# Differential attention's last rounds: p's parts, the key copies, the order of the end, and two weight splits

## The chip, the cores and the metric

The kernel runs on one core of one Trainium2 chip. The metric is the device time of one execution in microseconds. The kernel before has a median of 1311.96 us over three runs (1311.76 to 1312.21). Engines are named as in the profile: PE is TensorE, DVE is VectorE, ACT is ScalarE, POOL is GpSimd, SP is SyncE, which issues nearly all transfers here.

## The reference, cut to what matters

The program is a decoder trunk of two layers over 512 tokens of 1024 features. Layer 0 mixes tokens with a convolution, layer 1 with differential attention; each layer ends with a SwiGLU feed-forward part and a gated input embedding made from `p`. The change touches layer 1's attention, the projection of `p[1]`, and the first products with `w_o`:

```python
qkv = x @ w_qkv                                   # x is rms-normed
q = rms_norm(q per head half, q_g) * HEAD_DIM ** -0.5
k = rms_norm(k per head half, k_g)                # 8 heads, 2 halves (c) of 64
logits = einsum('bhcqd,bhckd->bhcqk', q, k) + bias, causal
w = softmax(logits)[c=0] - lam * softmax(logits)[c=1]
o = rms_norm(w @ v, sub_g) * (1 - lambda_init)    # per head, 128 wide
h = h + o @ w_o
...
h = h + sigmoid(rms_norm(h) @ ple_w_gate) * (p[1] @ ple_w_proj)
```

## The kernel before, in words

**Precision by parts.** Every operand of a large product is held as two fp32r parts, hi and lo, with hi + lo equal to the fp32 value. `mm3` (L153) makes a product of three matmuls: lo by hi, hi by lo, hi by hi. The parts of a weight come from `weight` (L138): SP loads a 128x1024 tile into `wraw` (two buffers), ACT copies it to `whi` (L149), and DVE, or POOL where `eng=G` is given, subtracts to make `wlo` (L150). `whi` and `wlo` have four buffers each, so at most four weights are ready at one time, and a buffer of `wraw` is free only when its subtraction is done.

**Order.** Instructions are written in program order; a planner with its own simulated times then decides in which order each engine gets them. Program order is the priority: an instruction written later may overtake where an earlier one isn't expected to be ready, and when a tile's buffer isn't free the instructions that need it wait. Once planned, each engine works through its queue in order. SP's queue holds the loads in the same way: a load that waits for a buffer of `wraw` holds back those behind it.

**Queries, keys, values.** Six slabs of four weights each (the table `QKV`, L81) run in the order q0, v0, q1, q2, v1, q3. A slab does four token blocks of 128 (`tb`); each block is 24 matmuls of 128x512 (`tokens`, L675). A value block is stored in its own tile `B0` to `B7` (`values`, L691): `B0` and `B1` are the first two blocks of heads 0 to 3. A q slab holds a pair of heads: after the block, ACT, DVE and POOL work out the norms (`unit`, L702), and one block later `unit_end` (L724) transposes on PE and writes the parts. For each half `c`, ACT writes the query's hi part (L735) and the key's hi part (L736) to 64 partitions, and then POOL copies the key's hi part to the other 64 partitions (L740, `KDUP = "G"`); DVE writes the two lo parts (L743, L745). The parts of a pair lie in tiles `C0` to `C5`, with two buffers each, so pairs 0 and 2 share one buffer, and pairs 1 and 3 the other.

**Attention.** The work of head `hd` and query block `qb` has three stages: `stage_s` (L752: scores on PE, L772 and L773; bias and minimum on DVE, L775; exponential on ACT, L779; three DVE steps L782 to L784), `stage_t` (L787: PE transposes L792, ACT and DVE make the parts L794 and L795) and `stage_a` (L801: products with the values L808 and L809; after the last block of a head the norm of the head, with POOL steps at L214 and L830). Round n holds the scores of item n, the transposes of item n-2, and the products of item n-3; there are 32 items, so rounds 0 to 34. `stage_o` (L834) transposes a finished head (L837) and splits it into `A` tiles. 63 of the 96 stages are placed between the matmuls of the six slabs (`pace`); 33 are left, from the last stage of round 22 on.

**The end of attention.** After the slabs, `pfeatures` (L249) loads the two halves of `p[1]` through `wraw` and writes their parts to tiles `C0` and `C1` (L253 on ACT, L254 on DVE). Then `project` (L259) makes the eight blocks of `p @ ple_w_proj`, six matmuls each, with two weights. Then `linear` (L537) does `o @ w_o`, the first two weights side by side over the eight heads. A call of `step()` (L873) takes one stage, and `stage_o` where a head is due; it stands before each block of `project`, twice inside it, and after each `mm3` of the first two `w_o` weights. These hooks are the arguments `before` and `after` of `linear`.

Of the kernel before, what the change touches and what calls it, by code (L numbers as in the profile page):

```python
# [13 lines left out]
F32R = mybir.dt.float32r  # L14
AF = mybir.ActivationFunctionType
# [5 lines left out]
P = 128  # L21
S = 512
D = 1024
NC = D // P
NH = 8
# [44 lines left out]
        TAPS += [(_c, j) for j in range(0, PE_TAPS[_c], 4)]  # L70


KDUP = "G"
HALVES = slice(0, DH), slice(DH, P)
LT = 2
LA = 3
# [8 lines left out]
def trunk(ctx, tc, xT, pT, wts, diag, dww, vec, rel, onehot, lamv, out):  # L85
    nc = tc.nc
    V, A, G, T = nc.vector, nc.scalar, nc.gpsimd, nc.tensor
# [7 lines left out]
    def sb(shape, tag, bufs, dt=F32):  # L95
        uid[0] += 1
        return pool.tile(shape, dt, tag=tag, name=f"{tag}_{uid[0]}", bufs=bufs)

    def ps(tag, bufs, shape=(P, S)):
        uid[0] += 1  # L100
        return psum.tile(list(shape), F32, tag=tag, name=f"{tag}_{uid[0]}", bufs=bufs)

    mm = lambda: ps("mm", 4)
# [4 lines left out]
    f = lambda ap: ap.bitcast(F32)  # L108
# [6 lines left out]
    def col(name, i=0):  # L115
        a, _ = VEC[name]
        return vt[:, a + i : a + i + 1]
# [7 lines left out]
    t = wk()[:, 0:P]  # L125
# [4 lines left out]
    t = tp()  # L130
# [7 lines left out]
    def weight(n=1024, pieces=1, between=(), eng=V):  # L138
        i = wnext[0]
        wnext[0] += 1  # L140
        raw = sb([P, 1024], "wraw", 2)
        hi = sb([P, 1024], "whi", 4, F32R)
        lo = sb([P, 1024], "wlo", 4, F32R)
        for k in range(pieces):
            cut = slice(k * n // pieces, (k + 1) * n // pieces)
            loaded[0] = nc.sync.dma_start(raw[:, cut], wts[i, :, cut])
            if k < len(between):
                between[k]()
            A.copy(hi[:, cut], raw[:, cut])  # L149
            eng.tensor_tensor(lo[:, cut], raw[:, cut], f(hi[:, cut]), ALU.subtract)  # L150
        return hi, lo

    def mm3(acc, a, b, first, last):  # L153
        (ah, al), (bh, bl) = a, b
        T.matmul(acc, al, bh, start=first, stop=False)  # L155
        T.matmul(acc, ah, bl, start=False, stop=False)  # L156
        return T.matmul(acc, ah, bh, start=False, stop=last)  # L157

    def wpart(w, k):
        return tuple(t[:, k * P : (k + 1) * P] for t in w)  # L160

    def both(t):
        return t[:, 0], t[:, 1]
# [4 lines left out]
    def split_scaled(src, scale, hi, lo):  # L168
        A.activation(hi, src, AF.Copy, scale=scale)  # L169
        V.scalar_tensor_tensor(lo, src, scale, f(hi), ALU.mult, ALU.subtract)  # L170
# [78 lines left out]
    def pfeatures(layer, parts):  # L249
        for k, (hi, lo) in enumerate(parts):  # L250
            raw = sb([P, 1024], "wraw", 2)[:, :S]
            nc.sync.dma_start(raw, pT[layer, :, k * S : (k + 1) * S])
            A.copy(hi, raw)  # L253
            (G if layer == 0 else V).tensor_tensor(lo, raw, f(hi), ALU.subtract)  # L254
        return parts

    ph = pfeatures(0, [(sb([P, S], t, 2, F32R), sb([P, S], t, 2, F32R)) for t in ("wth", "wtl")])

    def project(ph, m, w, o, step=lambda: None):  # L259

        acc = mm()
        for k in range(2):
            mm3(
                acc,
                wpart(w, 2 * (m % 4) + k),
                ph[k],
                k == 0,
                k == 1,
            )
            step()  # L270
        A.copy(o, acc)
        return o
# [239 lines left out]
    pp = []  # L512
    for m in range(NC):
        if m % 4 == 0:
            w = weight()
        with tc.issue_after((last_tap if m < 4 else last_moment)[0].ins):
            if m < 6:
                o = sb([P, S], f"D{m}", 1)
            elif m == 6:
                o2 = sb([P, 2, S], "C4", 2)  # L520
                o = o2[:, 0]
            else:
                o = o2[:, 1]
# [10 lines left out]
            if c >= 2:  # L534
                V.tensor_tensor(z[c - 2][1], y[c - 2], f(z[c - 2][0]), ALU.subtract)

    def linear(n_in, src, consume, group0=1, before=None, after=None, first=0):  # L537


        m = 0  # L540
        while m < NC:
            g = group0 if m == 0 else 1
            ws = [weight(n_in * P, eng=G if m == 0 and i >= g - first else V) for i in range(g)]
            accs = [mm() for _ in range(g)]
            for k in range(n_in):
                if before:
                    before(k)
                for w_, a_ in zip(ws, accs):
                    mm3(a_, wpart(w_, k), src[k], k == 0, k == n_in - 1)
                    if after:  # L550
                        after()
            for i in range(g):
                consume(m + i, accs[i])
            m += g
# [3 lines left out]
    def add_conv(m, acc):  # L558
        V.scalar_tensor_tensor(h[m], acc, col("b_pw2", m), h[m], ALU.add, ALU.add)
        norm.chunk(m)  # L560

    linear(NC, z, add_conv, 3, first=ZW)


# [73 lines left out]
    for k in range(2):  # L638
        t = tp()
# [27 lines left out]
    def slab(n=0):  # L667
        ws = [weight(eng=G if i < n else V) for i in range(4)]
        return [
            tuple(t[:, j * S : (j + 1) * S] for t in ws[k])  # L670
            for k in range(4)
            for j in range(2)
        ]
# [50 lines left out]
    def unit_end(pair, tb, q):  # L724
        t = tp()
        for i in range(4):
            T.transpose(t[:, i * P : (i + 1) * P], q[:, i * P : (i + 1) * P], ident)
        t4 = t.rearrange("p (h c t) -> p h c t", h=2, c=2)
        cut = slice(tb * P, (tb + 1) * P)
        qs, ks, kl = qk[pair][0:2], qk[pair][2:4], qk[pair][4:6]  # L730

        qg, kg = gains[:, 0:1], col("k_g")
        for c in range(2):
            own, other = HALVES[c], HALVES[1 - c]
            A.activation(qs[c][own, :, cut], t4[own, :, 0], AF.Copy, scale=qg[own])  # L735
            A.activation(ks[c][own, :, cut], t4[own, :, 1], AF.Copy, scale=kg[own])  # L736
            if KDUP == "A":
                A.activation(ks[c][other, :, cut], t4[own, :, 1], AF.Copy, scale=kg[own])
            else:
                G.tensor_copy(ks[c][other, :, cut], f(ks[c][own, :, cut]))  # L740
        for c in range(2):
            own, other = HALVES[c], HALVES[1 - c]
            V.scalar_tensor_tensor(  # L743
                qs[c][other, :, cut], t4[own, :, 0], qg[own], f(qs[c][own, :, cut]), ALU.mult, ALU.subtract)
            V.scalar_tensor_tensor(  # L745
                kl[c][own, :, cut], t4[own, :, 1], kg[own], f(ks[c][own, :, cut]), ALU.mult, ALU.subtract)
# [85 lines left out]
    ot = {}  # L832

    def stage_o(hd):  # L834
        t = tp()
        for i in range(4):
            T.transpose(t[:, i * P : (i + 1) * P], osb[hd][:, i * P : (i + 1) * P], ident)  # L837
        hi = sb([P, S], f"A{2 * hd}", 1, F32R)
        lo = sb([P, S], f"A{2 * hd + 1}", 1, F32R)
        split_scaled(t, gains[:, 1:2], hi, lo)  # L840
        ot[hd] = (hi, lo)
# [3 lines left out]
    stages = []  # L845
    for n in range(len(todo) + LA):
        for stage, at in ((stage_s, n), (stage_t, n - LT), (stage_a, n - LA)):
            if 0 <= at < len(todo):
                stages.append((n, partial(stage, *todo[at])))

    def take(n):
        got, stages[:n] = [s for _, s in stages[:n]], []
        return got

    waiting = None
    for what, at, pace in QKV:
        ws = slab(GLO if at > 0 else 0)
        for tb in range(4):
            between = take(3 * pace[tb])
            between += [None] * (6 - len(between))  # L860
            if waiting:
                between.append(partial(unit_end, *waiting))
                waiting = None
            if what == "v":
                values(at, ws, tb, between)
            else:
                waiting = unit(at, ws, tb, between)
    unit_end(*waiting)


    done = [0]

    def step():  # L873
        if stages:
            n, s = stages.pop(0)
            s()
        else:
            n = 99
        while done[0] < NH and (n - LA - 3) // 4 > done[0]:
            stage_o(done[0])  # L880
            done[0] += 1

    ph = pfeatures(1, [both(sb([P, 2, S], t, 2, F32R)) for t in ("C0", "C1")])
    pp = []
    for m in range(NC):
        if m % 4 == 0:
            w = weight()
        step()
        if m < 2:
            o = sb([P, S], f"D{m + 2}", 1)  # L890
        elif m % 2 == 0:
            o2 = sb([P, 2, S], f"C{m // 2 + 1}", 2)
            o = o2[:, 0]
        else:
            o = o2[:, 1]
        pp.append(project(ph, m, w, o, step))

    def heads_until(k):
        while done[0] <= k:
            step()  # L900

    norm = Norm("ffn_g1")

    def add_attn(m, acc):
        V.tensor_tensor(h[m], acc, h[m], ALU.add)
        norm.chunk(m)

    linear(NC, ot, add_attn, 2, heads_until, step)
    n2 = Norm("ple_g1")
    ffn(norm, n2)  # L910

# [131 lines left out]
```

## Time and profile before

| what | value |
|---|---|
| median of 3 runs | 1311.96 us (1311.76 to 1312.21) |
| the profiled execution's own time | 1313.88 us |
| its span in the trace, first to last instruction | 1312.1 us |
| PE busy, PEld busy | 1276.4 us (97%), 1047.4 us (80%) |
| DVE, ACT, POOL busy | 759.3, 526.9, 276.1 us |
| mean granted TensorE clock | 0.988 |
| data moved | 129.21 MB, 98 GB/s mean |

The profiled execution lies 1.92 us above the median, and 1.78 us above its own span. A row of the stage table gives the stretch of the span, its length, and the busy time of each engine with the number of its instructions in brackets; PEclk is the clock granted to TensorE as a share of full speed. In a row of the timeline stand the start, the duration, the engine, the line, the operation and the tiles; what stands in square brackets is the idle time of the engine just before, and who ended it. PE's busy time is modelled and overlaps, so that the distance from one matmul to the next, and not its duration, is what it costs.

### The profile page before, as it was taken

How to read it: one execution, taken by the hardware profiler on the slowest of the kernel's cores; microseconds unless marked ns; L12 is line 12 of the kernel's file. 1: busy time of each engine (PE TensorE's matmuls, PEld its weight loads, DVE VectorE, ACT ScalarE, POOL GpSimd, SP SyncE). 2: the span in 40 equal slices, each digit the busy share in tenths (PEclk: the TensorE clock that was granted, in tenths of full speed). 3: DMA queues.
4: the chain of work that ended last, by engine and by line, in shares of the span. 5: the costliest groups of instructions: out<-in, count | busy, mean ns of one | idle time of the engine just before them, and what ended most of it. 6: DMA issues, size and time to landing. Idle time of an engine off the chain costs nothing. (4 is left out here: it accounts for less than half of the span.)

```text
span 1312.1 us, 15285 instructions
## 1 busy us (share of the span) xinstructions
PE 1276.4 (97%) x5830; PEld 1047.4 (80%) x5830; DVE 759.3 (58%) x1168; ACT 526.9 (40%) x832; POOL 276.1 (21%) x219
## 2 busy tenths in 40 slices
PE   8999889999999999999999998999999999999998
PEld 5787668888888888888888886778888888888887
DVE  6998866544344434455678888945543344334445
ACT  5644255332123212253566767734332233223332
POOL 4839533000000000022345534122000000000030
PEclk8999889999999999999999998999999999999999
DMA  5554203332333232232222221213233323222231
GB/s 193 182 179 156 81 32 113 96 97 80 113 96 96 81 112 96 77 116 94 72 97 81 86 75 49 97 33 128 97 96 97 96 97 97 96 96 88 80 122 64
DMA packets 44534, 129.21 MB, mean 98 GB/s; under 512 B 5123, under 2 KB 8835, under 8 KB 44460
## 3 DMA queue, kind: packets, MB, share of 16 engines
q1 hardware_dynamic: 42912, 125.84, 29.2%
q10 hardware_dynamic: 1548, 2.39, 0.6%
q8 instruction: 46, 0.75, 0.2%
q14 instruction: 28, 0.23, 0.1%
HBM read 124.52 MB, written 3.69 MB: 98 GB/s over the span
## 5 line engine op out<-in xcount | busy, mean ns | idle before, releaser
L149 ACT CAST whi<-wraw 128x1024 fp32r<-128x1024 f32 (+2 forms) x214 | 218.5, 1026 | 563.5 <-PE mm L157 363.1
L155 PE MATMUL mm<-A,wlo 128*128 128x512 f32 (+1 forms) x1096 | 425.6, 392 | 9.5 <-ACT A L533 5.9
L156 PE MATMUL mm<-A,whi 128*128 128x512 f32 (+1 forms) x1096 | 428.9, 392 | 0.7 <-DVE A L170 0.5
L157 PE MATMUL mm<-A,whi 128*128 128x512 f32 (+1 forms) x1096 | 426.5, 390 | 0.0
L150 DVE TENSOR_TENSOR wlo<-wraw,whi 128x1024 fp32r<-128x1024 f32 (+2 forms) x207 | 257.5, 1248 | 66.6 <-ACT whi L149 66.2
L155 PEld LDWEIGHTS mm<-A,wlo 128*128 128x128 f32 x1096 | 207.2, 189 | 55.2 <-ACT A L533 6.7
L156 PEld LDWEIGHTS mm<-A,whi 128*128 128x128 f32 x1096 | 207.0, 189 | 48.0 <-DVE A L170 3.8
L157 PEld LDWEIGHTS mm<-A,whi 128*128 128x128 f32 x1096 | 207.0, 189 | 43.3 <-issue 1.3
L189 POOL TENSOR_TENSOR acc<-acc,wk 128x512 f32<-128x512 f32 x42 | 68.6, 1634 | 786.7 <-issue 673.3
L156 PE MATMUL mm<-B,whi 128*128 128x512 f32 x352 | 137.5, 391 | 0.0
L157 PE MATMUL mm<-B,whi 128*128 128x512 f32 x352 | 137.5, 391 | 0.0
L155 PE MATMUL mm<-B,wlo 128*128 128x512 f32 x352 | 137.1, 391 | 0.0
L591 DVE TENSOR_TENSOR h<-mm,h 128x512 f32<-128x512 f32 x48 | 33.0, 691 | 123.1 <-PE mm L157 123.0
L583 DVE TENSOR_TENSOR big<-mm,rb 128x512 f32<-128x512 f32 x44 | 30.4, 691 | 126.2 <-PE mm L157 126.2
L581 DVE TENSOR_TENSOR big<-mm,rb 128x512 f32<-128x512 f32 x44 | 30.4, 691 | 99.0 <-PE mm L157 92.6
L157 PEld LDWEIGHTS mm<-B,whi 128*128 128x128 f32 x352 | 66.1, 188 | 14.5
L156 PEld LDWEIGHTS mm<-B,whi 128*128 128x128 f32 x352 | 66.0, 188 | 14.3
L155 PEld LDWEIGHTS mm<-B,wlo 128*128 128x128 f32 x352 | 66.1, 188 | 14.2
L157 PE MATMUL mm<-whi,A 128*128 128x512 f32 x192 | 75.6, 395 | 0.0
L156 PE MATMUL mm<-wlo,A 128*128 128x512 f32 x192 | 75.0, 396 | 0.0
L155 PE MATMUL mm<-whi,A 128*128 128x512 f32 x192 | 74.8, 396 | 0.0
L214 POOL TENSOR_TENSOR r<-v,mhalf 128x8 f32<-128x8 f32 (+1 forms) x31 | 47.4, 1530 | 114.6 <-DVE v L212 92.4
(207 smaller groups left out, 1439.0 us busy)
## 6 DMA issues: line engine op xcount, KB each, us to landing
wraw<-in_wts SPq DMA_DIRECT2D x194, 512.0 KB, 3.5
wraw<-in_wts SPq DMA_DIRECT2D x16, 384.0 KB, 2.9
D<-in_diag SPq DMA_DIRECT2D x19, 256.0 KB, 4.7
C<-in_diag SPq DMA_DIRECT2D x12, 256.0 KB, 5.5
h<-in_xT SPq DMA_DIRECT2D x8, 256.0 KB, 5.3
bias<-scr ACTq DMA_DIRECT2D x8, 256.0 KB, 3.5
out_t<-h SPq DMA_DIRECT2D x7, 256.0 KB, 2.0
wraw<-in_wts SPq DMA_DIRECT2D x4, 256.0 KB, 4.8
```

The lines of the kernel that those rows point to most:

```text
L149: A.copy(hi[:, cut], raw[:, cut])
L150: eng.tensor_tensor(lo[:, cut], raw[:, cut], f(hi[:, cut]), ALU.subtract)
L155: T.matmul(acc, al, bh, start=first, stop=False)
L156: T.matmul(acc, ah, bl, start=False, stop=False)
L157: return T.matmul(acc, ah, bh, start=False, stop=last)
L189: self.eng.tensor_tensor(self.acc, self.acc, sq, ALU.add)
L214: last_pow[0] = G.tensor_tensor(r[:, :n], v[:, :n], mhalf[:, :n], ALU.pow)
L581: V.tensor_tensor(tg, pg, rb, ALU.mult)
L583: V.tensor_tensor(tu, pu, rb, ALU.mult)
L591: V.tensor_tensor(h[m], acc, h[m], ALU.add)
```

## The change

Four edits, all in layer 1's attention.

1. The parts of `p[1]` go into tiles `B0` and `B1` in place of `C0` and `C1`, and `pfeatures` is called when the slab q3 has been written down (`at == 3`), in place of after all slabs.
2. `unit_end` copies the key's hi part to the other 64 partitions by a transfer issued on ACT's queue, in place of a POOL copy; 32 of them, 64x256 fp32 each (64 KB).
3. The end of attention is written down in rounds. First the two weights of the projection (`pw`) and the first two of `w_o` (`wo`) are asked for. Then each round gives all its stages, the `stage_o` that is due, and one filler: two blocks of the projection, five heads of the first two `w_o` sums, two blocks of the projection. After the last round follow `stage_o(7)`, the other four blocks, and heads 5 to 7 of the two sums. `linear` then begins with the third weight.
4. The `wlo` of those first two `w_o` weights is made on POOL (`eng=G`) in place of DVE.

```diff
-    def linear(n_in, src, consume, group0=1, before=None, after=None, first=0):
-        m = 0
+    def linear(n_in, src, consume, group0=1, first=0, start=0):
+        m = start
...
-                if before:
-                    before(k)
                 for w_, a_ in zip(ws, accs):
                     mm3(a_, wpart(w_, k), src[k], k == 0, k == n_in - 1)
-                    if after:
-                        after()
...
             A.activation(ks[c][own, :, cut], t4[own, :, 1], AF.Copy, scale=kg[own])
-            if KDUP == "A":
-                A.activation(ks[c][other, :, cut], t4[own, :, 1], AF.Copy, scale=kg[own])
-            else:
-                G.tensor_copy(ks[c][other, :, cut], f(ks[c][own, :, cut]))
+            nc.scalar.dma_start(f(ks[c][other, :, cut]), f(ks[c][own, :, cut]))
...
         ws = slab(GLO if at > 0 else 0)
+        if at == 3:
+            ph = pfeatures(1, [both(sb([P, 2, S], f"B{k}", 1, F32R)) for k in range(2)])
...
-    done = [0]
-    def step():
-        if stages:
-            n, s = stages.pop(0)
-            s()
-        else:
-            n = 99
-        while done[0] < NH and (n - LA - 3) // 4 > done[0]:
-            stage_o(done[0])
-            done[0] += 1
-    ph = pfeatures(1, [both(sb([P, 2, S], t, 2, F32R)) for t in ("C0", "C1")])
+    pw = [weight(), weight()]
+    wo = [weight(eng=G), weight(eng=G)]
     pp = []
-    for m in range(NC):
-        if m % 4 == 0:
-            w = weight()
-        step()
+    oaccs = []
+    def factor():
+        m = len(pp)
...
-        pp.append(project(ph, m, w, o, step))
-    def heads_until(k):
-        while done[0] <= k:
-            step()
+        pp.append(project(ph, m, pw[m // 4], o))
+    def first_sums(k):
+        if k == 0:
+            oaccs.extend([mm(), mm()])
+        for w_, a_ in zip(wo, oaccs):
+            mm3(a_, wpart(w_, k), ot[k], k == 0, k == NC - 1)
+    fill = [factor] * 2 + [partial(first_sums, k) for k in range(5)] + [factor] * 2
+    done = 0
+    while stages:
+        n = stages[0][0]
+        for s in take_to(n + 1):
+            s()
+        while done < NH and (n + 1 - LA - 3) // 4 > done:
+            stage_o(done)
+            done += 1
+        if fill and (not hasattr(fill[0], "args") or fill[0].args[0] < done):
+            fill.pop(0)()
+    stage_o(NH - 1)
+    for _ in range(NC - len(pp)):
+        factor()
+    for k in range(5, NH):
+        first_sums(k)
...
-    linear(NC, ot, add_attn, 2, heads_until, step)
+    for m in range(2):
+        add_attn(m, oaccs[m])
+    linear(NC, ot, add_attn, start=2)
```

`take_to(n)` is a new helper that takes all stages of the rounds below n off the list.

More of the change, by code (lines that the diff above doesn't have):

```diff
@@ L70 @@
         TAPS += [(_c, j) for j in range(0, PE_TAPS[_c], 4)]
-KDUP = "G"
 HALVES = slice(0, DH), slice(DH, P)
@@ L849, in trunk, with take_to @@
                 stages.append((n, partial(stage, *todo[at])))
+    def take_to(n):
+        got = [s for at, s in stages if at < n]
+        del stages[: len(got)]
+        return got
     def take(n):
@@ L891, in trunk @@
         elif m % 2 == 0:
-            o2 = sb([P, 2, S], f"C{m // 2 + 1}", 2)
-            o = o2[:, 0]
-        else:
-            o = o2[:, 1]
-        pp.append(project(ph, m, w, o, step))
-    def heads_until(k):
-        while done[0] <= k:
-            step()
+            o2[0] = sb([P, 2, S], f"C{m // 2 + 1}", 2)
+            o = o2[0][:, 0]
+        else:
+            o = o2[0][:, 1]
+        pp.append(project(ph, m, pw[m // 4], o))
+    o2 = [None]
+    def first_sums(k):
[19 more added lines that the diff above has]
+        first_sums(k)
     norm = Norm("ffn_g1")
```

## The prediction

> **What bounds the kernel now.** I read the engine shares first, then the stages around the change, then the waits inside the bad ones.
>
> ```profile
> PE 1276.4 (97%) x5830; PEld 1047.4 (80%) x5830; DVE 759.3 (58%) x1168; ACT 526.9 (40%) x832; POOL 276.1 (21%) x219
> ...
> core 0: us, PE busy (x) PEld busy (x) DVE busy (x) ACT busy (x) POOL busy (x), PEclk, DMA share, GB/s
> 655.00:806.00 151.00, 148.73 (x779) 126.19 (x778) 120.82 (x313) 100.40 (x229) 74.17 (x71) 1.00 0.23 76
> 806.00:812.00 6.00, 4.02 (x24) 3.03 (x22) 5.80 (x14) 5.58 (x14) 1.29 (x3) 1.00 0.00 0
> 812.00:823.20 11.20, 6.95 (x23) 5.94 (x24) 10.96 (x31) 8.34 (x21) 5.67 (x6) 0.54 0.60 189
> 823.20:832.00 8.80, 6.86 (x35) 4.81 (x34) 8.02 (x20) 7.02 (x15) 1.95 (x1) 1.00 0.43 149
> 832.00:859.90 27.90, 27.69 (x173) 24.51 (x171) 22.32 (x69) 18.32 (x48) 4.09 (x4) 1.00 0.12 39
> 872.00:878.00 6.00, 3.47 (x18) 2.40 (x15) 3.84 (x6) 3.77 (x6) 0.00 (x0) 1.00 0.00 0
> 1000.00:1100.00 100.00, 100.00 (x441) 82.50 (x440) 43.12 (x50) 26.70 (x32) 0.00 (x0) 1.00 0.31 100
> ```
>
> PE is the bound of the whole, at 97%, so only time in which PE stands or runs slowly can be won. The slabs (655 to 806) leave it 151.00 - 148.73 = 2.27 us. Their end is the bad place. From 806 to 832 PE stands 1.98 + 4.25 + 1.94 = 8.17 us, and between 812 and 823.2 its granted clock is 0.54, so its 6.95 busy us do the work of 3.75: another 3.2 us. From 832 to 859.9 it stands 0.21 us, from 872 to 878 it stands 2.53 us. Together 14.1 us: the ceiling of this change. DVE is nearly full there (10.96 of 11.20 us), so a hole that is filled may leave DVE as the next bound. The last row gives a matmul of 512 columns: 100.00 / 441 = 0.227 us; one filler (six of them) is 1.36 us.
>
> Why PE had nothing to do shows in the buffers of the loads.
>
> ```profile
> L252 SPq DMA_DIRECT2D wraw<-in_pT x2: 327/328/328, 781.3 to 783.3; - x2
> L253 ACT CAST C<-wraw x2: 637/638/638, 809.0 to 809.5; 128x512 fp32r<-128x512 f32 x2
> L254 DVE TENSOR_TENSOR C<-wraw,C x2: 679/680/680, 812.2 to 813.1; 128x512 fp32r<-128x512 f32 x2
> ...
> 812.89 8.05 SPq L146 DMA_DIRECT2D wraw<-in_wts  x4
> 816.88 1.04 ACT L149 CAST whi<-wraw 128x1024 fp32r<-128x1024 f32 x1 [2.06 <-DMA wraw<-in_wts]
> 818.10 1.22 DVE L150 TENSOR_TENSOR wlo<-wraw,whi 128x1024 fp32r<-128x1024 f32 x1
> 819.75 0.78 PE L155 MATMUL mm<-C,wlo 128*128 128x512 f32 x1
> ```
>
> The two halves of p were loaded at 781.3 and 783.3, but their casts waited for tiles C0 and C1, a buffer that pair 2 holds until its last scores, so they ran at 809. For 29 us they held both buffers of wraw, and SP's next weight was issued only at 812.89. The projection, PE's filler for these rounds, began at 819.75.
>
> **Part 1, p's parts in B0 and B1.** These tiles are free after the products of head 3 (round 18, within slab v1), before p's loads. Casts and subtractions move to the landing, near 786: 2 x 0.64 us ACT and 2 x 0.68 us DVE go into the slabs, where DVE has 30 us free of 151: cost nothing, or 1.4 us were DVE full there. SP's next weights are then issued near 789, in place of 812.89; the two projection weights wait for whi until the last slab's weights come free, about 802 to 806, so the first factor can start near 806 and not 819.75.
>
> **Part 2, the written end.** What is late next is DVE.
>
> ```profile
> 806.00:859.90 53.90, 45.52 (x252) 38.30 (x250) 47.09 (x131) 39.26 (x93) 13.01 (x14) 0.91 0.26 84
> ...
> 806.00:859.90 53.90, 7.49 (x6) 0.00 (x0) 0.91 0.26 84
> ```
>
> The first row is the stretch to DVE's last transposed parts, the second DVE's weight subtractions in it: six, 1.25 us each. DVE is busy 47.09 us. Out of the stretch go p's 1.36, the projection's two subtractions 2.50 (now ready before), w_o's first two 2.50 (to POOL) and w_o's fourth 1.25 (its buffer now comes free after the last factor): 7.6 us, which leaves 39.5. Its 6.8 idle us were waits for scores and exponentials; I keep half, 3.4, since PE's late filler caused some of them; the bounds are none and all. With the 3.6 us that part 4 adds, attention's rounds end near 806 + 39.5 + 3.6 + 3.4 = 852.5 in place of 859.9, 7.4 us earlier (849.1 to 855.9).
>
> PE's work from 806 to 878 is 72.0 - 14.1 = 57.9 us at full speed. Of it 16 fillers are 21.8 and w_o's third and fourth weight (48 matmuls) 10.9, so 25.2 is attention. By 852.5 PE can have done attention and nine fillers, 37.5 us of 46.5; the other 9 us take the four late factors (5.4) if the planner pulls them forward. That it does so shows here:
>
> ```profile
> 864.88 0.22 PE L809 MATMUL mm<-B,wtl 128*128 128x128 f32 x1
> 873.20 0.75 DVE L170 SCALAR_TENSOR_TENSOR A<-tp,lam,A 128x512 fp32r<-128x512 f32 x1 [3.90 <-ACT A L169]
> 873.22 1.19 PE L155 MATMUL mm<-A,wlo 128*128 128x512 f32 x4 [0.78 <-ACT A L169]
> 874.92 2.00 ACT L149 CAST whi<-wraw 128x1024 fp32r<-128x1024 f32 x2 [1.75 <-PE mm L157]
> 876.72 1.22 DVE L150 TENSOR_TENSOR wlo<-wraw,whi 128x1024 fp32r<-128x1024 f32 x1
> 877.99 0.50 PE L155 MATMUL mm<-A,wlo 128*128 128x512 f32 x1 [1.75 <-DVE wlo L150]
> ```
>
> Four w_o sums stood open for head 7 at 873.22: two had been pulled forward. So all four ended together, the fifth weight found no free whi before 874.92, and PE stood 1.75 us for it after 0.78 for head 7; in the new order the sums end one after another, and both waits go. Behind the last round then stand 3 fillers and 48 matmuls, 15.0 us; head 7's chain (864.88 to 873.95, 9.1 us) lies beside 2 fillers and the two weights' first seven heads, 12.3 us. End: 852.5 + 15.0 = 867.5 against 878.0, a gain of 10.5 us; without the pulling forward the four factors come behind, and it is 5.1. I take 9, nearer to the first because of the row above. Two sums now hold two of the four accumulators from round 24; factors and value products share two, and a drain is short beside a round of 3 to 4 us: nothing.
>
> **Part 3, keys by transfers.**
>
> ```profile
> L740 POOL CAST C<-C x32: 389/397/1281, 660.4 to 821.0; 64x256 fp32r<-64x256 f32 x32
> ...
> 803.30 0.46 ACT L735 ACTIVATE C<-tp,lam 64x256 fp32r<-64x256 f32 x1
> 803.65 0.46 ACT L736 ACTIVATE C<-tp,vec 64x256 fp32r<-64x256 f32 x1
> ...
> L647 ACTq DMA_DIRECT2D bias<-scr x8: 326/326/455, 647.6 to 812.0; - x8
> ...
> DMA to landing us min/median/max: 3.0/3.5/4.0
> ```
>
> POOL loses 32 copies of 0.40 us, off the path. ACT gains 32 issues. No row shows an issue that waits for the activation before it. ACT starts its next activation 0.35 us after the last (803.30, 803.65); an issue takes 0.33, and waiting for the key's end gives up 0.11 of overlap: 0.44 us each at most, nothing where the other half's query activation lies between. What is queued behind it on ACT is the other half's parts and the exponentials. 28 copies lie in the slabs: 0 to 12.3 us of ACT, on top of 100.40 of 151. PE was full there with 50 us of ACT free, but the planner's order on each engine is fixed, so local waits grow: I take 1.5 us of PE, bounds -0.3 (waits on POOL that go) and 12.3. The four in the end add 0 to 1.8, I take 0.6. The copy lands some 3.5 us after its issue, by the nearest row, in place of 0.40; the scores that read it follow its block by a block or more (24 matmuls, 5.4 us): nothing, or up to 3.1 us for each of three later pairs, 9.3.
>
> **Part 4, two splits on POOL.**
>
> ```profile
> 681.17 2.40 POOL L150 TENSOR_TENSOR wlo<-wraw,whi 128x1024 fp32r<-128x1024 f32 x1 [6.19 <-issue]
> 682.01 2.64 DVE L150 TENSOR_TENSOR wlo<-wraw,whi 128x1024 fp32r<-128x1024 f32 x1 [1.13 <-ACT whi L149]
> ...
> 710.51 2.38 POOL L150 TENSOR_TENSOR wlo<-wraw,whi 128x1024 fp32r<-128x1024 f32 x1
> 710.71 3.20 DVE L212 TENSOR_SCALAR v<-v 128x8 f32<-128x8 f32 x1
> ...
> 740.16 2.39 POOL L150 TENSOR_TENSOR wlo<-wraw,whi 128x1024 fp32r<-128x1024 f32 x1
> 740.39 2.19 DVE L212 TENSOR_SCALAR v<-v 128x4 f32<-128x4 f32 x1 [0.46 <-POOL r L214]
> ...
> 772.08 2.41 POOL L150 TENSOR_TENSOR wlo<-wraw,whi 128x1024 fp32r<-128x1024 f32 x1 [2.87 <-issue]
> 773.54 0.97 DVE L825 TENSOR_TENSOR v<-v,r 128x4 f32<-128x4 f32 x1
> 774.54 0.16 DVE L826 TENSOR_TENSOR v<-v,r 128x4 f32<-128x4 f32 x1
> 774.74 0.17 DVE L212 TENSOR_SCALAR v<-v 128x4 f32<-128x4 f32 x1
> ```
>
> A split leaves DVE (1.25) but holds DVE up: in four cases a DVE step stretched by 2.64 - 1.22 = 1.4, 3.20 - 0.17 = 3.0, 2.0 and 0.8 us, mean 1.8. Two splits: 3.6 us against 2.5 saved. The edit by itself is a loss of 1.1 us.
>
> [...]
>
> **The sum.** -9 (parts 1, 2 and 4) + 1.5 + 0.6 = -6.9 us. The profiled execution, 1313.88 us, becomes 1307.0; the median stands 1.92 below it: 1305.0.
>
> **Rivals.** *PE never stands* (12%): DVE keeps none of its waits and the planner fills each hole; all 14.1 us come back: 1297.9. For it: PE has 16 independent fillers. Against: DVE at 98% in the worst stretch. *The lock eats the gain* (12%): w_o's splits fall in the rounds where DVE binds, each with a POOL norm step behind it as at 710 (3.0 us each, 6.0), DVE keeps its 6.8 idle us and the factors stay behind: rounds end at 806 + 39.5 + 6.0 + 6.8 = 858.3, PE at 878.7, and the time is 1312.7 and with part 3 1314.8: no change, or the edge of it. *ACT becomes the bound* (18%, the other side): each key issue holds ACT for 0.44 us in a queue that exponentials share; 32 are 14 us. The rest gains 9 us, so this decides where more than 65% of the 14 reaches PE; in full, or with scores that wait for landings as well, the time is near 1317. For it: ACT is busy 13.9 of 17.2 us from 806 to 823.2; against: 100.40 of 151 in the slabs.
>
> **The chances.** The forecast's own case has 58%, 1301 to 1309. The range from 1298 to 1316 leaves about 2 in 10 outside: it takes in the ceiling and most of the slower case. About 0.2% (2.6 us) is what a measurement can tell from no change. Faster: 58 + 12, less the forecast's thin edge, 0.69; the same: most of the lock's case and that edge, 0.12; slower: 0.19.
>
> **What would show it.** Right: the parts of p are made near 786; weights issued near 789; the first factor near 806; granted clock 1.00 in the rounds; rounds over near 852; no wait for the fifth w_o weight. Wrong: ACT idle before or after its key issues with PE waiting on scores in the slabs; DVE steps of 2 us or more beside POOL's two splits; PE at half clock in a late round without filler.

## The result and the profile after

The changed kernel takes 1322.3 us (median of six runs, 1316.64 to 1323.61), the kernel before 1312.11 beside it (six runs, 1311.76 to 1313.13): a ratio of 1.0071, 95% interval 1.0054 to 1.0089. It is 9.3 us slower where 7 us less were forecast, and outside the range. Five of the six runs lie from 1321.66 to 1323.61 us at a mean granted clock of 0.983 or 0.984, the sixth at 1316.64 with 0.988. Its profiled execution took 1323.61 us, with a span of 1321.5, 9.4 longer than before. In its lines the steps named in the prediction have line numbers that are 1 to 8 lower: the weight split is L149, the matmuls of `mm3` are L154 to L156, scores L764, the softmax's two combining steps L775 and L776.

The stretches of PE are those shown of before (us, PE busy, PEld, DVE, ACT, POOL, then clock, DMA share, GB/s).

```profile
655.00:806.00 151.00, 147.13 (x755) 123.91 (x754) 122.96 (x307) 98.75 (x226) 58.57 (x42) 0.98 0.30 93
806.00:812.00 6.00, 6.00 (x35) 5.17 (x34) 5.87 (x14) 5.92 (x12) 1.69 (x2) 1.00 0.24 52
812.00:823.20 11.20, 6.10 (x32) 4.81 (x30) 10.45 (x24) 7.74 (x19) 7.81 (x5) 0.81 0.47 161
823.20:832.00 8.80, 6.23 (x19) 4.31 (x20) 7.65 (x20) 3.43 (x9) 2.95 (x3) 0.50 0.28 83
832.00:859.90 27.90, 25.07 (x141) 20.88 (x140) 22.43 (x74) 18.69 (x48) 3.48 (x3) 0.93 0.01 1
859.90:872.00 12.10, 12.10 (x63) 10.58 (x63) 4.87 (x14) 5.05 (x10) 2.24 (x3) 0.86 0.14 43
...
745.00:750.00 5.00, 2.64 (x12) 2.16 (x13) 4.97 (x13) 2.89 (x9) 1.62 (x2) 0.73 0.15 34
750.00:755.00 5.00, 5.00 (x15) 3.96 (x15) 4.55 (x13) 3.66 (x9) 4.65 (x4) 0.59 0.56 206
```

Two places lost. In the slabs PE stands 3.87 us instead of 2.27, and at a clock of 0.98 its 147.13 busy us do 2.9 us less work: together some 4.5 us, most of it at 745. In the end the hole is as deep as before: from 806 to 832 PE stands 7.67 us (8.17 before), and its last 6.23 busy us there run at half clock. From 832 to 859.9 it has become worse (2.83 us of standing, 0.21 before). The timeline shows what lay at both places.

```profile
743.59 2.36 POOL L149 TENSOR_TENSOR wlo<-wraw,whi 128x1024 fp32r<-128x1024 f32 x1
743.68 2.82 DVE L776 SCALAR_TENSOR_TENSOR big<-rb,st,big 128x512 f32<-128x512 f32 x1
746.89 0.33 PE L764 MATMUL sc<-C,C 128*128 128x128 f32 x1 [2.03 <-DVE st L767]
...
814.86 2.38 POOL L149 TENSOR_TENSOR wlo<-wraw,whi 128x1024 fp32r<-128x1024 f32 x1 [1.87 <-ACT whi L148]
815.65 2.01 DVE L776 SCALAR_TENSOR_TENSOR big<-acc,st,big 128x384 f32<-128x384 f32 x1
818.65 0.39 PE L764 MATMUL sc<-C,C 128*128 128x256 f32 x1 [1.78 <-DVE st L767]
820.36 2.34 POOL L149 TENSOR_TENSOR wlo<-wraw,whi 128x1024 fp32r<-128x1024 f32 x1
820.87 1.85 DVE L775 SCALAR_TENSOR_TENSOR st<-st,lam 128x1 f32<-128x1 f32 x1
822.66 1.04 POOL L716 TENSOR_TENSOR big<-big,r 128x512 f32<-128x512 f32 x1
822.75 1.50 DVE L776 SCALAR_TENSOR_TENSOR big<-rb,st,big 128x512 f32<-128x512 f32 x1
824.81 0.69 PE L764 MATMUL sc<-C,C 128*128 128x384 f32 x1 [4.39 <-DVE C L735]
```

Each of the three weight splits on POOL lies over a DVE step of the softmax, and that step is stretched (2.82, 2.01, 1.85 us). The fourth long step, 1.50 us at 822.75, lies over POOL's norm step (L716), which ran right behind the last split. PE then waits for a DVE step that is queued behind the stretched one: twice for the read of earlier scores (L767), and at 824.81 for the lo part of a query (L735). The pair at 814 and 820 is part 4's. The one at 743 was in the kernel before too, at 740.16, where it lay beside a small step of the norm (the 2.19 us row at 740.39 that the prediction quotes). Nothing in the diff names it.

### The profile page after: what moved, and what is told of

It is laid out like the page before. It is cut to its first block, busy times and chain, and to the rows that moved or that the text cites. A ratio compares the mean times of both kernels' runs of the same rounds, so it can differ in the third digit from the quotient of the medians.

```text
span 1321.5 us, 15286 instructions
## 1 busy us (share of the span) xinstructions
PE 1282.5 (97%) x5830; PEld 1050.9 (80%) x5830; DVE 763.8 (58%) x1166; ACT 527.6 (40%) x832; POOL 265.7 (20%) x189
## 4 chain that ended last, share of the span: by engine, by line
PE 81%; DVE 8%; issue 3%; POOL 2%; ACT 1%; DMA 1%; SPq 0%; ACTq 0%; POOLq 0%; DVEq 0%
PE mm L154 26%; PE mm L155 26%; PE mm L156 26%; POOL wk L390 2%; DVE sc L401 2%; DVE wlo L149 2%; PE mm L800 1%; PE sc L764 1%; PE sc L765 1%; PE tp L784 1%; PE tp L722 1%; DVE big L776 0%; DVE B L401 0%; PE tp L829 0%; ACT C L389 0%
## 5 line engine op out<-in xcount | busy, mean ns | idle before, releaser
L154 PE MATMUL mm<-A,wlo 128*128 128x512 f32 (+1 forms) x1096 | 425.1, 393 | 10.6 <-ACT A L532 5.9
L156 PE MATMUL mm<-A,whi 128*128 128x512 f32 (+1 forms) x1096 | 427.6, 390 | 0.0
L149 DVE TENSOR_TENSOR wlo<-wraw,whi 128x1024 fp32r<-128x1024 f32 (+2 forms) x205 | 255.8, 1251 | 69.6 <-ACT whi L148 69.2
L154 PEld LDWEIGHTS mm<-A,wlo 128*128 128x128 f32 x1096 | 207.3, 190 | 57.0 <-ACT A L532 6.8
L156 PEld LDWEIGHTS mm<-A,whi 128*128 128x128 f32 x1096 | 207.7, 189 | 43.5 <-issue 1.3
L154 PE MATMUL mm<-B,wlo 128*128 128x512 f32 x368 | 143.5, 392 | 0.4 <-ACT C L270 0.4
L155 PE MATMUL mm<-B,whi 128*128 128x512 f32 x368 | 143.7, 390 | 0.0
L156 PE MATMUL mm<-B,whi 128*128 128x512 f32 x368 | 143.7, 390 | 0.0
L154 PEld LDWEIGHTS mm<-B,wlo 128*128 128x128 f32 x368 | 69.1, 188 | 15.3 <-ACT C L270 0.5
L156 PEld LDWEIGHTS mm<-B,whi 128*128 128x128 f32 x368 | 69.1, 188 | 15.2
L155 PEld LDWEIGHTS mm<-B,whi 128*128 128x128 f32 x368 | 69.1, 188 | 14.7
L154 PE MATMUL mm<-whi,A 128*128 128x512 f32 x192 | 76.8, 405 | 0.0
L156 PE MATMUL mm<-whi,A 128*128 128x512 f32 x192 | 76.2, 398 | 0.0
```

## The experiments

Theories: **L**, POOL's splits hold DVE up where PE waits for it (the lock: a name for what the rows show, a softmax step of 128x512 of 2.82 us beside a split, where the mean of eight in the kernel before is 0.75; what in the chip makes it isn't shown); **K** or **A**, the key transfers cost by themselves (ACT's issues, or their landing); **O**, the written order leaves PE without filler. In the expectations, **D** is the landing of the last four copies, u4 is the first run below, and av0 the whole change with no split on POOL. Differences in us below are (ratio - 1) x 1312.5, each ratio against the kernel before on the same chip; 0.1% is 1.3 us.

### One part at a time

The change with w_o's splits back on DVE:

```diff
-    wo = [weight(eng=G), weight(eng=G)]
+    wo = [weight(), weight()]
```

> The changed kernel with one part undone: the first two w_o weights are split on DVE again. [...] Theory K (the key copies and the plan they cause are the loss): 1320 to 1323, the slabs keep their 3.9 us of standing PE. Theory O (the written order leaves PE without filler whatever DVE does): 1319 to 1323, with the hole at the same place.

That, and the keys copied by POOL again (parts 1 and 2 are left):

```diff
-            nc.scalar.dma_start(f(ks[c][other, :, cut]), f(ks[c][own, :, cut]))
+            G.tensor_copy(ks[c][other, :, cut], f(ks[c][own, :, cut]))
```

> The changed kernel with two parts undone: w_o's splits on DVE and the keys copied by POOL; p's parts in B0 and B1 and the written order stay. Theory L: as without the splits on POOL, 1311 +- 3. Theory K: the slabs' 4.5 us come back, 1317. L and K together: 1306 +- 3, what I had forecast for parts 1 and 2. Theory O: 1318 or more.

The kernel before with part 1 alone:

```diff
         ws = slab(GLO if at > 0 else 0)
+        if at == 3:
+            ph = pfeatures(1, [both(sb([P, 2, S], f"B{k}", 1, F32R)) for k in range(2)])
...
-    ph = pfeatures(1, [both(sb([P, 2, S], t, 2, F32R)) for t in ("C0", "C1")])
```

> The kernel before with part 1 alone: p's parts in B0 and B1, made during the last slab. If the buffers of the loads were the cause of the hole, the projection begins near 806 and not 819.75, and the time falls by 4 to 9 us, to 1303 to 1308. If DVE, full at that place, is the bound anyway, under 2.6 us: 1309.5 to 1312.

And with part 3 alone (the diff of the keys, the other way round):

> The kernel before with part 3 alone: the keys copied by transfers on ACT's queue. Theory K: PE stands about 2 us longer in the slabs and runs some 3 us of work at half clock, 1316 +- 2. Theories L and O: 1312 +- 1.5; each issue is hidden behind the other half's activation.

Measured: 1317.8 (1.0041, 1.0026 to 1.0056), 1316.42 (1.0026, 1.0016 to 1.0036), 1314.04 (1.0010, 1.0001 to 1.0020), 1320.54 (1.0060, 1.0045 to 1.0075). The first lies between L's 1311 +- 3 and the ranges of K and O, the second near K's 1317, the third above both of its ranges, the fourth above K's. Part 3 alone costs 7.9 us, nearly the whole loss; but taken out of the change (the first run against the second) it wins back only 2.0, so the parts act on each other. Part 1 alone brings nothing, though its filler comes early. First its stretches of PE (columns as above), then, from its timeline, the first factor:

```profile
806.00:812.00 6.00, 4.75 (x29) 3.94 (x28) 5.83 (x10) 5.41 (x12) 1.33 (x2) 1.00 0.33 102
812.00:823.20 11.20, 6.39 (x31) 4.80 (x29) 10.07 (x31) 6.24 (x17) 4.56 (x5) 0.83 0.37 119
823.20:832.00 8.80, 6.07 (x23) 4.17 (x23) 7.13 (x20) 6.90 (x17) 1.83 (x3) 0.63 0.00 0
832.00:859.90 27.90, 27.69 (x170) 24.35 (x169) 22.32 (x70) 18.43 (x48) 4.09 (x4) 1.00 0.12 39
```

```profile
807.37 0.44 PE L155 MATMUL mm<-B,wlo 128*128 128x512 f32 x1
```

The hole comes all the same. Of the eight factors only three run by 816; the other five start at 833.73, where they started before (833.50). The sums of the first two are copied out only at 829.49 and 830.72 (829.01 and 830.66 before): their output tiles D2 and D3 hold heads 2 and 3 until `stage_o` has transposed them, which comes after the slabs. That these two sums, which keep two of the four accumulators, hold the five back is argued from the kernel and these times; no run changes it alone. From 832 on the rows are those of before, and PE is full there (27.69 of 27.90 us).

### What in part 3 costs

The 28 copies of the slabs by transfer and the last four on POOL; then the reverse:

```diff
+            if pair == 3 and tb >= 2:
+                G.tensor_copy(ks[c][other, :, cut], f(ks[c][own, :, cut]))
+            else:
                 nc.scalar.dma_start(f(ks[c][other, :, cut]), f(ks[c][own, :, cut]))
```

> The kernel before with the 28 key copies of the slabs made by transfers from ACT's queue; the last four (pair 3, blocks 2 and 3) stay copies on POOL. Part 3 alone took +7.6 us, and I read some 4.5 us of it from the slabs (PE hole near 745 to 750 and half clock after) and some 3 us from the end (a score that stood 6.00 us for a copy). If the price is in the slabs and in the end separately: +4.5 us (3.5 to 5.5), 1317.4. Theory D, that nearly all is the landing of the last four: +1 us or less. Theory A, that it is ACT's time for issues, in proportion to their number: 28/32 of 7.6 = +6.7 us.

> The counterpart: the 28 copies of the slabs stay on POOL, only the last four (pair 3, blocks 2 and 3) are transfers. By the split above: +3 us (2 to 4), 1315.9, with slabs as before (2.3 us of PE idle from 655 to 806) and a score that waits some 6 us for a copy near 818 to 824. Theory D: +6.5 us or more. Theory A: 4/32 of 7.6 = +1 us.

Part 3 with no split of the slabs on POOL, and the kernel before with the same line changed:

```diff
-GLO = 1
+GLO = 0
```

> Part 3 alone, and besides, none of the slabs' weight splits on POOL (they go to DVE). [...] Theory A (issues hold up ACT): the hole stays or moves, and the distance to the kernel with POOL copies stays at 7 us or more.

> The kernel before with none of the slabs' weight splits on POOL, the base of the run above. PE idled only 2.3 us in the slabs, and DVE has 30 us free there; a split on DVE costs it 1.2 us where POOL's held it up by 1.8 on average (four cases): no change by either theory, 1312.9 within 1.5 us. If it comes out faster by more than 1.5 us, the lock took time in the kernel before as well.

Measured: 1319.52 (1.0050, 1.0031 to 1.0068), 1315.1 (1.0014, 1.0005 to 1.0024), 1313.48 (1.0006, 0.9992 to 1.0020), 1313.25 (1.0000, 0.9988 to 1.0012). So 6.6 us lie in the slabs and 1.8 in the end. These two alone would fit theory A, by which the price goes with the number of transfers (6.7 and 1). But without POOL's splits part 3 costs 0.8 us, which isn't told from none, and ACT still issues 32 transfers there: theory A falls. The wait of some 6 us for a copy, expected where only the last four are transfers, isn't in that run.

Then part 3 with one of the four splits, in the slab of v's second half, on DVE:

```diff
-        ws = slab(GLO if at > 0 else 0)
+        ws = slab(GLO if at > 0 and (what, at) != ("v", 1) else 0)
```

> Part 3 alone, and of the four weight splits that POOL makes in the slabs one, in the slab of v's second half, is made by DVE. In the trace of part 3 alone that one (744.63, 2.37 us) lies beside a DVE step of the softmax of 2.82 us, and PE stands 4 us around it and then runs at half clock; the other three lie beside other splits and the norm's small steps, as in the kernel before. Theory L (this one collision carries the slabs' loss): the hole at 745 and the half clock after it are gone, PE idle from 700 to 750 is 2 us or less, and of the 7.6 us some 5 to 7 come back: 1314.9 (1313.5 to 1316). Theory A (issues on ACT, or landings): one split more or less changes nothing, 1319 to 1321.

1313.16 (1.0002, 0.9992 to 1.0013): the one instruction, with all that follows from it, carries 7.6 of the 7.9 us, somewhat more than expected. The two timelines are the same up to it, 0.7 us apart. Part 3 alone, its timeline (here L781 is the softmax step, L769 a score):

```profile
744.63 2.37 POOL L150 TENSOR_TENSOR wlo<-wraw,whi 128x1024 fp32r<-128x1024 f32 x1
744.72 2.82 DVE L781 SCALAR_TENSOR_TENSOR big<-rb,st,big 128x512 f32<-128x512 f32 x1
747.93 0.33 PE L769 MATMUL sc<-C,C 128*128 128x128 f32 x1 [2.02 <-DVE st L772]
```

With that split on DVE, the timeline:

```profile
744.02 0.75 DVE L781 SCALAR_TENSOR_TENSOR big<-rb,st,big 128x512 f32<-128x512 f32 x1
744.69 1.22 DVE L150 TENSOR_TENSOR wlo<-wraw,whi 128x1024 fp32r<-128x1024 f32 x1
...
774.24 2.38 POOL L150 TENSOR_TENSOR wlo<-wraw,whi 128x1024 fp32r<-128x1024 f32 x1
774.33 2.44 DVE L781 SCALAR_TENSOR_TENSOR big<-acc,st,big 128x128 f32<-128x128 f32 x1
```

and the stretch after 750 with that split on DVE:

```profile
750.00:806.00 56.00, 55.96 (x304) 47.69 (x303) 47.47 (x130) 38.79 (x94) 22.71 (x17) 1.00 0.24 75
```

The step takes 0.75 us instead of 2.82. The two rows at 774 are a correction to what I expected: another split meets a softmax step there, 2.44 us where the shape's mean in the kernel before is 0.40, and it costs nothing, because PE has matmuls of the slab to do meanwhile (the stretch: 55.96 of 56.00 us busy, clock 1.00). The same 2 us of DVE go with some 7 us of time at one place and with none at another.

The two profiled executions lie 5.0 us apart in span (1319.1 and 1314.1), as the one with the split on DVE took 1316.2 us, 3 above its median. And something else differs between them: in part 3 alone a score of the last rounds waits for a key copy, and with the split on DVE it doesn't. From the waits of part 3 alone (us in total, times, longest):

```profile
PE sc L769 <- DMA C<-C: 6.0, 1, 6.0
```

This wait can't be most of the price. The run with 28 transfers in the slabs doesn't have it and costs 6.6 us; part 3 with `GLO = 0` has it and costs 0.8.

### Part 4, and the whole change without the lock

Part 4 alone in the kernel before:

```diff
-    linear(NC, ot, add_attn, 2, heads_until, step)
+    linear(NC, ot, add_attn, 2, heads_until, step, 2)
```

> Part 4 alone, in the kernel before with its own order: w_o's first two weights split on POOL. Theory L: each of the two holds up a DVE step for up to 2.4 us where DVE binds: +1 to +4.5 us (4.5 is what the two cost in the whole change), 1314 to 1317.4. My prediction's price for this part, 3.6 us of hold-up against 2.5 saved: +1.1 us. A rival, that the price is the written order's alone, because there the splits fall in the rounds: 0 within 1 us, since in the order of before they come later.

1311.99 (0.9996, 0.9986 to 1.0005): nothing. In the order of before the two splits come later, and lie over a step of a head's norm and a read of scores, as its timeline shows. That nothing which binds PE waits behind those steps is argued from the time:

```profile
821.28 2.40 POOL L150 TENSOR_TENSOR wlo<-wraw,whi 128x1024 fp32r<-128x1024 f32 x1 [1.33 <-ACT whi L149]
821.60 2.10 DVE L828 TENSOR_TENSOR r<-r,r 128x4 f32<-128x4 f32 x1
...
824.78 2.37 POOL L150 TENSOR_TENSOR wlo<-wraw,whi 128x1024 fp32r<-128x1024 f32 x1
825.27 0.55 DVE L775 CUSTOM_DVE_ANT_0 acc<-sc,bias 128x384 f32<-128x384 f32 x1
...
826.46 0.70 DVE L783 SCALAR_TENSOR_TENSOR st<-st,lam 128x1 f32<-128x1 f32 x1
```

The whole change with no split on POOL (`GLO = 0`, and w_o on DVE):

> The whole change with no weight split on POOL at all, neither in the slabs nor of w_o: parts 1 to 3 and DVE for all splits. Theory L: what parts 3 and 4 cost goes (7.6 and 4.5, less what they shared), and the written order's +3.3 (parts 1 and 2 together) is what stays: 1316.2 (1313 to 1317.5). If transfers of keys cost anything besides the lock, it is more, up to the 1317.8 of the same kernel with the slabs' splits on POOL.

Part 1 alone with `GLO = 0`:

> A candidate: p's parts early (part 1 alone, +1.1 us) and no weight splits on POOL (alone 0: the slabs ended 2.2 us earlier, and PE stood 3.8 us from 806 to 812 for want of filler, since SP's weight came at 814). With the filler there early the two should add up: 1310.5 (1308 to 1313). If instead the rounds after 812 are bound by their own chain of scores, softmax and transposes, whatever fills PE: 1313 to 1314, and the rows from 832 on are those of the kernel before again.

The whole change with the one split of v on DVE; with `GLO = 0` but w_o's splits on POOL; parts 1 and 2 with `GLO = 0`; and the first of these with w_o on DVE:

> The whole change, with one of the slabs' four POOL splits (v's second half) on DVE; w_o's two stay on POOL. If that one collision costs here what it cost in part 3 alone (7.4 us): 1322.3 - 7.4 = 1314.9 (1312 to 1317). If the loss of the change lies in its end instead, in w_o's splits and the order: 1319 or more.

> The whole change, none of the slabs' splits on POOL, w_o's two still there. Against the same with w_o's on DVE (1309.45) it prices part 4 in the written order. Theory L: the two splits lie in the rounds where DVE binds, 4.5 us as between the change and u4: 1314 (1312.5 to 1315.5). Rival: part 4 costs nothing, as alone in the kernel before: 1309.5 (1308 to 1311), and the 4.5 us were another difference of place.

> Parts 1 and 2 (keys copied by POOL as before, w_o split on DVE), none of the slabs' splits on POOL. Against the same with key transfers (1309.45) it prices part 3 without the lock; against parts 1 and 2 with the slabs' splits on POOL (+3.3 us) it shows whether the lock was in that +3.3 too. If transfers do nothing by themselves (as in the kernel before, 1313.5 against 1313.3): 1309.5 (1308 to 1311). If the gain of av0 comes from the transfers: 1313 or more.

> The change with w_o on DVE (1317.8) and v's second half's split on DVE; three splits of the slabs stay on POOL. If that one split is all that matters in the slabs: 1310 (1308.5 to 1312), as with no POOL splits at all (1309.45). If the other three cost too: 1313 to 1315.

Measured:

| run | median, us | ratio, 95% interval |
|---|---|---|
| the whole change, no split on POOL | 1309.45 | 0.9975 (0.9966 to 0.9985) |
| part 1 alone, `GLO = 0` | 1312.29 | 0.9998 (0.9988 to 1.0007) |
| the whole change, v's split on DVE | 1317.12 | 1.0036 (1.0021 to 1.0051) |
| the whole change, `GLO = 0`, w_o's splits on POOL | 1313.2 | 1.0003 (0.9993 to 1.0013) |
| parts 1 and 2, `GLO = 0` | 1312.64 | 0.9998 (0.9989 to 1.0008) |
| the whole change, v's split and w_o's on DVE | 1313.35 | 1.0006 (0.9996 to 1.0015) |

Part 1 with `GLO = 0` gains nothing although its slabs end 2 us earlier: its row from 832 to 859.9 has 27.69 busy us again, as before. Without POOL's splits the whole change is faster than the kernel before, by 3.3 us, where 4 us slower was expected. The slabs' four splits cost it 8.9 us (1.0071 against 1.0003), the one of v 4.6 of them; the other three cost 4.3, which I hadn't expected. Where they do isn't shown: PE's busy time from 655 to 806 differs by only 1.5 us (148.81 with the three on POOL, 150.32 with none). W_o's two cost 3.7 (1.0003 against 0.9975), although alone they cost nothing. And key transfers gain 3.0 us here (0.9998 against 0.9975), where alone they gained none.

### The written order

The best variant without the order: parts 1 and 3, `GLO = 0`, the end as in the kernel before.

> Parts 1 and 3 in the order of the kernel before, no weight split on POOL in the slabs (w_o on DVE): the best variant (1309.45) less the written order. If the order brings that gain: 1312.5 to 1313.5, as the other variants with the old order and no POOL splits (1312.3, 1313.25, 1313.5). If the order costs (the +2.4 that it seemed to cost with the splits on POOL): 1307 to 1308.

And the best variant with its fillers in another order:

```diff
-    fill = [factor] * 2 + [partial(first_sums, k) for k in range(5)] + [factor] * 2
+    sums = [partial(first_sums, k) for k in range(5)]
+    fill = [factor, factor, sums[0], sums[1], factor, sums[2], factor, sums[3], factor, sums[4]]
```

> The best variant (1309.45: the whole change without splits on POOL), with the fillers written in another order: factors and w_o's sums take turns, so that six factors instead of four lie in the rounds. In its trace PE stood 2.26 us at 842 for head results that w_o's sum itself reads, 0.5 at 839, and ran at half clock after. If a filler that waits for nothing closes that stand: 1306.5 (1305 to 1308.5). If the sums are pulled forward by the planner all the same, or the factors come at the cost of the tail: 1309 to 1311.

1306.54 (0.9950, 0.9934 to 0.9967) and 1306.23 (0.9949, 0.9931 to 0.9967). With key transfers and no splits the order brings no gain, it costs 3.3 us (0.9950 against 0.9975): the opposite of what I had put first. That isn't a fixed price: with keys copied by POOL and no splits of the slabs there, part 1 stands at 0.9998 without the order and at 0.9998 with it. Its own stand can be mended: in the variant with the change's order PE waits for head results that the filler itself reads; with factors between the sums the stretch from 832 has 2.1 us more work in it, and the time is that without the order. With the change's order: that stretch, the wait in the timeline, and the line of the last transposed parts (count, ns min/median/max, first and last start).

```profile
832.00:859.90 27.90, 24.46 (x130) 20.26 (x130) 17.37 (x54) 15.70 (x34) 7.21 (x6) 0.94 0.06 19
```

```profile
844.10 1.22 PE L154 MATMUL mm<-A,wlo 128*128 128x512 f32 x2 [2.26 <-ACT A L168]
```

```profile
L787 DVE TENSOR_TENSOR wtl<-tp,wth x32: 281/486/692, 680.6 to 849.6; 128x128 fp32r<-128x128 f32 x8, 128x256 fp32r<-128x256 f32 x8, 128x384 fp32r<-128x384 f32 x8, 128x512 fp32r<-128x512 f32 x8
```

With factors between the sums, the stretch:

```profile
832.00:859.90 27.90, 26.55 (x154) 22.66 (x153) 19.53 (x61) 16.84 (x40) 7.06 (x6) 1.00 0.12 38
```

Both last variants beat both kernels, by 6.6 us against the one before.

The account of the 9.3 us, from ratios: parts 1 and 3 -6.6, the written order +3.3, w_o's splits on POOL +3.7, the slabs' splits on POOL +8.9. It closes by construction, since each run differs from the next in one of these; in another sequence the parts would get other shares, as they act on each other.

## Why the prediction was wrong, point by point

**Part 1: right in time, wrong in worth.** The parts of p are made from 789.5 on (786 forecast), and the first factor comes at 807.37 with part 1 alone, as worked out (813.12 in the whole change, whose slabs end later). It was wrong to put PE's standing down to loads that came late. With the loads early only three of the eight factors come forward, the other five stay where they were (833.73), part 1 alone gains nothing, and 832 to 859.9 stays as it was. I had written that DVE might be the next bound, and took 9 us for the three parts all the same. In the changed kernel, the line of the casts of p, and that of the factors that run behind the rounds (first matmul of each half, two to a factor):

```profile
L252 ACT CAST B<-wraw x2: 619/622/624, 789.5 to 791.1; 128x512 fp32r<-128x512 f32 x2
```

```profile
L154 PE MATMUL mm<-B,wlo x8: 387/389/396, 865.1 to 872.1; 128*128 128x512 f32 x8
```

**Part 2: the rounds end where forecast only without POOL's splits, and the worth of the order was wrong.** Rounds were to end at 852.5. In the change their last transposed parts come at 864.6 (before: 859.2). Without the slabs' splits on POOL they come at 852.5, without any split on POOL at 849.6, and at 851.8 when the order is left out as well, so most of this isn't the order's doing. From there "a gain of 10.5 us" fails on "if the planner pulls them forward": four factors stayed behind the rounds (eight first matmuls from 865.1 to 872.1, above), while w_o's sums, taken as filler, waited for their heads. With key transfers and no splits the order costs 3.3 us. The wait for the fifth weight that was to go is there unchanged, as the waits of the changed kernel say (us in total, times, longest):

```profile
PE mm L154 <- DVE wlo L149: 1.8, 1, 1.8
```

**Part 3: the step that failed.** "POOL loses 32 copies of 0.40 us, off the path" was costed at nothing. With the copies gone, one of POOL's weight splits began at 744.63 instead of 740.16, beside the softmax instead of a small step of the norm, and with that split on DVE 7.6 of part 3's 7.9 us come back; in the whole change 4.6 do (1.0071 against 1.0036). The slabs' four splits on POOL, which cost nothing in the kernel before (1.0000 without them), are 8.9 us in the account above, a term that the sum of the prediction didn't have. That the planner moved the one at 744.63 because POOL's queue was shorter is argued from this, not traced. The terms that I did cost were small: 1.5 us of PE in the slabs for ACT's issues and 0.6 for the end. The issue itself is longer than the 0.44 us that I allowed for it, 0.60 in the row quoted below, and yet the part costs 0.8 us once the lock is gone (0.9992 to 1.0020). The landing is 2.0 us in the median, not 3.5.

**Part 4: the hold-up was right, its price was not.** Three stretched steps in the change: 2.01 instead of 0.62, 1.85 instead of 0.21, 1.50 instead of 0.75, together 3.8 us of DVE, where I had 3.6; the third was held by the norm step behind the split. But the price was put in DVE time, 1.1 us net. PE pays otherwise: 3.7 us in the written order, nothing in the old one. The rows of part 4 alone show that not every step beside a split is held: the one on the norm's `r` (L828, 128x4) took 2.10 us, where the mean in the kernel before is 0.16, while the one that reads scores (L775, 128x384) took 0.55 us in the middle of POOL's split, as long as in the kernel before. What decides it isn't shown: the step of 3.20 us that the prediction quotes at 710 names a single tile as its input. Nor do the holds end alike. Of the prediction's four stretched steps two end with POOL's split (740 and 772). At 710 the step ends at 713.91 with POOL's next one (L830, 712.85 to 713.88), and at 682 it ends 1.08 us after the split, nearly its own length of 1.22.

**The rivals.** "ACT becomes the bound" had 1317 for the time, and the wrong cause: part 3 with ACT's issues and without the lock loses 0.8 us, not told from none. "The lock eats the gain" had the right cause at the right place for w_o's two splits, but looked only there, and stopped at 1314.8; that the factors stay behind, as it had it, came true. **The range** took its upper end from these two; a mechanism that was already in the profile (four stretched steps, quoted) and could move was in none of them.

## What to carry to other kernels

Where an operation holds up another engine, its price depends on what it meets (some 2 us of DVE went with 7.6 us at 744 and with none at 774): before taking work off its queue, list the holding instructions and ask where each will lie afterwards, as a row that costs nothing today can move onto the critical chain. Price a hold-up in the time of the bounding engine at that place, its slower clock included, not in the time of the engine that is held (5.8 us against 2.07 in the rows of the next section). And test such a kernel's parts with the holding operation taken away first: alone, key transfers went from 7.9 us lost to a loss not told from none, and beside parts 1 and 2 they then gained 3.0.

## What the hardware showed beyond that

**A stand that cost twice.** A hold of 2.07 us on DVE (2.82 against 0.75) goes with 7.6 us of part 3's time. In these rows of part 3 alone, PE stands 2.74 of 5 us, and then works 5 us at half clock.

```profile
745.00:750.00 5.00, 2.26 (x14) 1.66 (x13) 4.97 (x7) 2.66 (x7) 2.00 (x1) 0.88 0.00 1
750.00:755.00 5.00, 5.00 (x16) 4.13 (x15) 4.59 (x14) 4.00 (x10) 4.47 (x4) 0.50 0.75 235
755.00:760.00 5.00, 5.00 (x29) 4.33 (x28) 4.00 (x8) 2.22 (x5) 0.84 (x1) 0.94 0.28 104
```

That is 2.7 for the stand and 0.3 + 2.5 + 0.3 for the clock, 5.8 us of work lost for 2.07 us of DVE; the rest of the 7.6 isn't in these rows. The longest single stand here was 2.02 us; the clock granted was 0.88, 0.50 and 0.94 in the three rows, and in the 5.00 us at 0.50 PE was at work throughout. What makes it fall isn't shown: from 872 to 878 in the kernel before PE stood 2.53 us too (0.78 and 1.75 of it for head 7 and the fifth weight), at a clock of 1.00 there and from 878 to 884.

**A small copy can land late.** The 64 KB copies land 2.0 us after issue in the median, but up to 7.0 in part 3 with `GLO = 0`. There two were issued just behind a bias load and two weight loads, and a score waited for them. That these loads delayed them is argued from the order of issue. The timeline of that kernel, and then the times to landing of its 32 copies:

```profile
808.38 0.33 ACTq L647 DMA_DIRECT2D bias<-scr  x1
808.54 1.14 SPq L146 DMA_DIRECT2D wraw<-in_wts  x2
808.75 0.60 ACTq L737 DMA_DIRECT2D C<-C  x1
809.45 0.60 ACTq L737 DMA_DIRECT2D C<-C  x1
815.18 0.66 PE L769 MATMUL sc<-C,C 128*128 128x384 f32 x1 [5.97 <-DMA C<-C]
```

```profile
DMA to landing us min/median/max: 2.0/2.0/7.0
```

**Two parts that only gain together.** With `GLO = 0` part 1 alone stands at 0.9998, part 3 alone at 1.0006, both at 0.9950. A piece of it can be read: with part 1 the weights are loaded earlier, and PE has no wait for a copy any more. Another: the five late factors start at 826.05, against 831.16 with part 1 alone and 831.77 with part 3 alone. That this is all of the 6 us isn't shown; the one run that would price it, copies that land late with nothing else changed, wasn't made.
